# A causal mask moved to another engine, keys and queries stored by head pairs: a two-layer attention trunk on one core

## The chip, the cores and the metric

The kernel runs on one core of a Trainium2 chip. The metric is the device time of one execution in microseconds (us), and the time of a kernel is the median over its runs. Where the text speaks of the span, that is the time from the first to the last instruction in the profile of one execution.

The engines are called as the profile calls them: PE (matrix products and transposes), PEld (PE's loading of weights), DVE (vector operations), ACT (activations and copies), POOL (a second vector engine), SP (which here only issues transfers). A small q behind a name (SPq) is the engine's sequencer, and an instruction there keeps no datapath busy.

## The reference, cut to what matters

Each of two layers is a pair of token mixers followed by a gated feed-forward part with a short convolution. The change lies in the mixers. Mixer B is stick-breaking attention over four heads of 64 channels and 1024 tokens:

```
z = (q @ k.T) * scale
causal = key_pos < query_pos                    # strictly
log_stay = where(causal, log_sigmoid(-z), 0)
later = reverse_cumsum(log_stay) - log_stay
attn  = where(causal, exp(log_sigmoid(z) + later), 0)
o     = attn @ v
```

So the weight of a key is beta = sigmoid(z) times the product of stay = sigmoid(-z) over all later keys. A masked key has beta 0 and stay 1. Mixer A is softmax attention with a bias that falls with distance: four "near" heads over a window of 128 tokens, and eight "far" heads with strides of 4 and 16. All products are in float32, made from high and low parts (hi, lo), three matmuls for a product of two full numbers.

## The kernel before, in words

**Two streams on PE.** In the mixer a class `Dense` holds the input projections (gates, keys, queries, values) as generators. One *dense step* is six matmuls of 512 columns. A function `attend` runs the attention items in order: sixteen *stick* items (four heads, and for each four blocks of 256 queries, longest first: block 3 down to 0), four *near* items, sixteen *far* items. After each micro-step of an item, `dense.advance(rate)` adds the rate to an account and runs a dense step for each whole one in it. The rates are RATE (by block of the stick item), RATE_N (near) and RATE_T (far). PE's order is the order in which the program writes it. The order on the other engines and on SP's queue is set by the framework's planner, from the times that it expects and from priorities (`high_priority(offset=AHEAD)` goes first); on the chip each engine and each queue then works strictly in that order.

**A stick item.** `score(a)` (L682) makes the scores of 128 queries against all keys up to theirs, in pieces of up to 512 columns, last keys first: two matmuls (L631, L632) into a bank `z` of tag "s", the mask added to the last 128 columns by DVE (L695), sigmoid into `beta` (L696) and sigmoid of the negative into `stay` (L697) on ACT. `scans` (L704) then runs DVE's product scan over `stay` (L710) and multiplies `beta` by it (L714). `turn` (L716) transposes `beta` on PE (L722, `sb_t`, tag "t") and splits the result into hi (`sbh`, ACT, L143) and lo (`sbl`, DVE, L150); `apply` (L726) multiplies with the values into `sb_o` (L735, tag "o"), and at the end of an item `fold` (L646, L647) reads it out. Each tag of banks ("ps", "s", "t", "o") has two buffers. The scores of the next item are made between the micro-steps of the current one. While the first stick items run, block sums for the projections (L1013 to L1022 and their splits) are made on the side.

**Keys and queries.** `pair_near` (L1160) projects the keys (c = 0) and queries (c = 1) of two heads at a time, in two token halves n. Each result is 128 rows (two heads of 64) by 512 tokens, hi and lo, and `keep_kq` (L574) writes it to DRAM: for a key four transfers, for a query six, since the hi part of a query is stored twice (on rows 0 to 63 and 64 to 127). `fetch_row` (L652) brings a block of 256 tokens of one head back with three transfers: keys (hi over lo, 128 rows), query hi (twice, 128 rows), query lo (64 rows); `fetch_whole` (L669) does the same for a near head. Values follow on their own (`fetch_values`). A stick item may start six dense steps (LEAD) after its head's last fetch was written down. For the far heads, `fetch_kq` (L841) brings keys and queries from `tk`; the first item may start LEAD = 6 steps after its fetch, the others LEAD_T = 3.

**Values.** `pair_v` (L1175) projects values channel-first and turns them on PE (L1181, `v_t`, tag "t"); ACT and DVE read the bank out (L1185, L1186).

**Pool.** In the mixer, Pool makes two sums of weight blocks for each pair of projections (L1083, L1084), as soon as the weights `in_a` have landed.

Of the kernel before, what the change touches and what calls it, by code (L numbers as in the profile page):

```python
# [7 lines left out]
F32 = mybir.dt.float32  # L8
F32R = mybir.dt.float32r
I32 = mybir.dt.int32  # L10
BF16 = mybir.dt.bfloat16
AF = mybir.ActivationFunctionType
ALU = mybir.AluOpType
# [3 lines left out]
P = 128  # L17
T = 1024
D = 1024
KD = D // P  # L20
HF = 512
# [19 lines left out]
IN_ORDER = {ET.PE, ET.Activation, ET.DVE, ET.Pool}  # L41
HEAD = 4
SECOND = 0.35
RATE = (1.15, 1.3, 1.4, 1.45)
RATE_N = 0.75
RATE_T = 0.5
PLAIN = 4
EARLY = 3
LEAD = 6
# [8 lines left out]
def f32(ap):  # L58
    return ap.bitcast(F32)
# [3 lines left out]
def trunk_kernel(ctx, tc, x, norm1, w_in, b_gate, w_br, w_o, norm2, w_up, conv_w, conv_b, w_down, norm_f, out, depth=None, probe=None):  # L63
# [16 lines left out]
    pool.memset(eps, EPS)  # L80
    zero = cp.tile([P, 1], F32, name="zero")
    pool.memset(zero, 0.0)
    mask_b = cp.tile([P, P], BF16, name="mask_b")
    base0 = cp.tile([P, 256], BF16, name="base0")
    base2 = cp.tile([P, 256], BF16, name="base2")

# [2 lines left out]
    def masks():  # L89

        t = [sb.tile([P, 256], F32, tag="pt", bufs=PT, name=f"msk{i}") for i in range(3)]
        pool.memset(t[0][:, 0:P], 0.0)
        pool.affine_select(t[0][:, 0:P], t[0][:, 0:P], [[-1, P]], ALU.is_gt, -FAR, base=0, channel_multiplier=1)
        dve.tensor_copy(mask_b, t[0][:, 0:P])
        pool.iota(t[1], [[-1, 256]], base=P, channel_multiplier=1, allow_small_or_imprecise_dtypes=True)
        pool.affine_select(t[1], t[1], [[-1, 256]], ALU.is_ge, FAR, base=P, channel_multiplier=1)
        pool.affine_select(t[2], t[1], [[1, 256]], ALU.is_ge, FAR, base=0, channel_multiplier=-1)
        dve.tensor_copy(base0, t[2])
        rem = sb.tile([P, 256], I32, tag="pt", bufs=PT, name="rem")
        pool.iota(rem, [[-1, 256]], base=256, channel_multiplier=1)  # L100
        one = dve.tensor_scalar(rem, rem, 3, None, ALU.bitwise_and)
        tc.add_manual_dep(one.ins, LAST["g0"], NO_SYNC, reason="in turn")
        dve.tensor_copy(t[0], rem)
        dve.tensor_scalar(t[0], t[0], FAR, None, ALU.mult)
        LAST["base"] = dve.tensor_tensor(base2, t[1], t[0], ALU.add).ins.name
# [13 lines left out]
    obd = dr.tile([P, 2, T], F32, name="obd")  # L119
    tk = [dr.tile([2, 4, P, 6, 256], F32, name=f"tk{i}") for i in range(2)]  # L120
    tv = [dr.tile([2, 4, P, 2, 256], F32, name=f"tv{i}") for i in range(2)]
    sk = [dr.tile([P, T], F32, name=f"sk{i}") for i in range(8)]
    sq = [dr.tile([P, 2, T], F32, name=f"sq{i}") for i in range(8)]
    sv = [dr.tile([P, KD, P], F32, name=f"sv{i}") for i in range(8)]
    dn = [dr.tile([4, T], F32, name=f"dn{i}") for i in range(2)]

    def bank(tag, name):
        return ps.tile([P, 512], F32, tag=tag, name=name)
# [95 lines left out]
    class Dense:  # L224
# [38 lines left out]
        def fetch(self):  # L263


            def there(i):
                return i < 16 and {"N11" if i else "N10", f"1{i // 8}", f"2{i // 8}"} <= self.done

            def there_v(i):
                return i < 16 and self.near == 4 and {"v1", "v2"} <= self.done  # L270

            def row(j):
                return j < 16 and f"K{j // 4}" in self.done and self.rows >= j - 3

            def row_v(j):
                return j < self.b and self.free[3 - j % 4] >= j // 4

            def whole(v):
                return v < 4 and self.b == 16 and self.rows == 16 and {f"K{4 + v}", f"V{4 + v}"} <= self.done and self.near >= v

            while row(self.b):
                fetch_row(self.b)
                self.at(LEAD, lambda j=self.b: self.done.add(f"FB{j}"))
                self.b += 1
            while row_v(self.bv):
                fetch_values(self.bv)
                self.bv += 1
            while whole(self.n):
                fetch_whole(self.n)
                self.at(LEAD_N, lambda v=self.n: self.done.add(f"FN{v}"))  # L290
                self.n += 1
            while self.kq < self.scored + 2 and there(self.kq):
                fetch_kq(self.kq)
                self.at(LEAD_T if self.kq else LEAD, lambda i=self.kq: self.done.add(f"F{i}"))
                self.kq += 1
            while self.v < self.applied + 4 and there_v(self.v):
                fetch_v(self.v)
                self.v += 1
# [274 lines left out]

    def keep_kq(c, n, u, hi, lo):  # L574

        t = slice(n * HF, (n + 1) * HF)
        for s in range(2):
            rows = slice(64 * s, 64 * s + 64)
            if c:
                for src, kind, up in ((hi, 0, 0), (hi, 0, 64), (lo, 1, 0)):  # L580
                    nc.sync.dma_start(sq[u + s][up : up + 64, kind, t], f32(src[rows]))
            else:
                for src, up in ((hi, 0), (lo, 64)):
                    nc.sync.dma_start(sk[u + s][up : up + 64, t], f32(src[rows]))

    def in_parts(c, scale, hi, lo, x):
        if c:
# [64 lines left out]
    def fetch_row(j):  # L652

        u, qp = j // 4, 3 - j % 4
        if j == 0:
            R["kv"] = sb.tile([P, 2, T], F32R, tag="xa", bufs=4, name="kv")
            R["slots"] = sb.tile([P, 4, 2, 256], F32R, tag="xa", bufs=4, name="slots")
            pool.memset(f32(R["slots"][64:128, :, 1, :]), 0.0)
        t = slice(256 * qp, 256 * qp + 256)
        nc.sync.dma_start(f32(R["kv"][:, 0, t]), sk[u][:, t])  # L660
        nc.sync.dma_start(f32(R["slots"][:, qp, 0, :]), sq[u][:, 0, t])
        nc.sync.dma_start(f32(R["slots"][0:64, qp, 1, :]), sq[u][0:64, 1, t])

    def fetch_values(j):
        u, qp = j // 4, 3 - j % 4
# [2 lines left out]

    def fetch_whole(v):  # L669
        kv = R["kvn", v] = sb.tile([P, 2, T], F32R, tag="xa", bufs=4, name="kv")  # L670
        nc.sync.dma_start(f32(kv[:, 0, :]), sk[4 + v])
        for k in range(2):
            up = (P, 64)[k]
            nc.sync.dma_start(f32(R["slots"][0:up, :, k, :]), sq[4 + v][0:up, k, :].rearrange("p (m c) -> p m c", c=256))
        nc.sync.dma_start(f32(kv[:, 1, :]).rearrange("p (b c) -> p b c", c=P), sv[4 + v])

    def stick_item(dense, u, qp):
# [4 lines left out]
        def score(a):  # L682
            L = P * (2 * qp + a + 1)
            bt = rows[a] = sb.tile([P, T], F32, tag="p4", bufs=4, name="beta")
            if a == 0:
                st[0] = sb.tile([P, 2, T], F32, tag="xa", bufs=4, name="stay")
            sv = st[0][:, a, :]
            for c1 in range(L, 0, -512):
                c0 = max(0, c1 - 512)
                w = c1 - c0  # L690
                z = bank("s", "z")
                scores(z[:, :w], *(q[:, x, a * P : a * P + P] for x in range(2)), k[:, c0:c1])
                with tc.high_priority(offset=AHEAD):
                    if c1 == L:
                        dve.tensor_tensor(z[:, w - P : w], z[:, w - P : w], mask_b, ALU.add)  # L695
                    act.activation(bt[:, c0:c1], z[:, :w], AF.Sigmoid)  # L696
                    act.activation(sv[:, c0:c1], z[:, :w], AF.Sigmoid, scale=-1.0)  # L697
                (SCANS if c1 == L else left).append((shared, bt, sv, c0, c1, L))
            if a:
                SCANS.extend(left)  # L700
                dense.rows += 1
                scans(2)
# [472 lines left out]
    def pair_v(dense, l, g):  # L1175


        def turn(c, n, f):
            tp = bank("t", "v_t")
            for r in range(4):  # L1180
                pe.transpose(tp[:, r * P : (r + 1) * P], f[:, r * P : (r + 1) * P], ident)  # L1181
            tw = tp.rearrange("p (r h c) -> p r h c", r=4, h=2)
            vv = sb.tile([P, 4, 2, P], F32R, tag="ot", name="vv")
            with tc.high_priority(offset=AHEAD):
                act.copy(vv[:, :, :, 0:64], tw)  # L1185
                dve.tensor_tensor(vv[:, :, :, 64:128], tw, f32(vv[:, :, :, 0:64]), ALU.subtract)  # L1186
            for h in range(2):
                if g:
                    there = tv[c][h, :, :, g - 1, n * P : (n + 1) * P].rearrange("r p c -> p r c")
                else:  # L1190
                    there = sv[4 + 2 * c + h][:, 4 * n : 4 * n + 4, :]
                nc.sync.dma_start(there, f32(vv[:, :, h, :]))
            if (c, n) == (1, 1):
                dense.done |= {f"v{g}"} if g else {f"V{u}" for u in range(4, 8)}

        def put(c, n, x, psum, room=None):
            f = x
            if psum:
                f = small("vf")
                act.copy(f.rearrange("p (r j) -> p r j", r=4) if g else f, x)  # L1200
            dense.at(5, lambda: turn(c, n, f))

        off = OFF_VA + 256 * g
        return pair(dense, l, (off, off + P), g > 0, put)
# [892 lines left out]
```

## Time and profile before

| | |
|---|---|
| median of three runs | 2689.2 us (2685.47, 2689.20, 2691.84) |
| profiled execution | 2686.16 us |
| its span | 2684.4 us |
| mean granted clock of PE | 0.996 |
| mixer of layer 1, stick, near, far items | from about 76, 361 and 445 us |
| mixer of layer 2, stick, near, far items | from about 1404, 1685 and 1768 us |

A row of the waits names an engine and what it waited for, with the total, the number of times and the longest in us. A row of a timeline gives start and duration in us, engine, line, operation, what is written and what is read, and in brackets the idle time before it and what ended that. A row of windows gives a stretch in us, the busy time of PE, PEld, DVE, ACT and POOL in it with the number of instructions, the granted share of PE's clock, the busy share of the transfer engines and GB/s. A row of transfers gives tensors, issuing queue, count, size and the median time from issue to landing in us.

### The profile page before, as it was taken

The numbers are of one execution on the slowest core, as the hardware profiler recorded it, in microseconds if no ns is written. First come the engines' busy times: TensorE is split into PE (matmuls) and PEld (weight loads), VectorE is DVE, ScalarE is ACT, GpSimd is POOL, SyncE is SP. The second block draws the span as 40 slices with busy tenths as digits, with TensorE's granted clock in tenths as the row PEclk, the third lists the DMA queues.
The fourth block names the chain that finished last, engine by engine and source line by source line (L and its number), as shares of the span: only waits on it lengthen the run. The fifth ranks groups of instructions, "written<-read, shape, count | busy, mean of one in ns | idle before, by whom it ended". The sixth has DMA issues, their size and how long they took to land.

```text
span 2684.4 us, 36762 instructions
## 1 busy us (share of the span) xinstructions
PE 2633.4 (98%) x12780; PEld 2198.9 (82%) x12780; DVE 2074.2 (77%) x3159; ACT 1340.2 (50%) x2488; POOL 677.0 (25%) x483
## 2 busy tenths in 40 slices
PE   9999999999999999999999999999999999999999
PEld 8787788888888888888888877878888888888888
DVE  6887766685888988897659777667958888898865
ACT  5455566574555554532435455655745555554225
POOL 5311011122233443321161101100321434344210
PEclk9999999999999999999999999999999999999999
DMA  8553587783244444688453546876732444446863
GB/s 259 147 143 112 146 217 211 236 274 111 78 134 157 160 146 149 223 316 321 160 163 91 150 117 164 224 221 223 251 94 72 161 153 146 160 157 250 333 246 121
DMA packets 418917, 482.94 MB, mean 180 GB/s; under 512 B 26420, under 2 KB 336044, under 8 KB 416940
## 3 DMA queue, kind: packets, MB, share of 16 engines
q1 hardware_dynamic: 418716, 480.59, 55.9%
q8 instruction: 101, 1.65, 0.3%
q14 instruction: 84, 0.69, 0.1%
q10 hardware_dynamic: 16, 0.00, 0.0%
HBM read 307.43 MB, written 173.08 MB: 179 GB/s over the span
## 4 chain that ended last, share of the span: by engine, by line
PE 77%; DVE 10%; ACT 3%; DMA 3%; issue 2%; SPq 1%; POOL 0%; DVEq 0%; ACTq 0%; POOLq 0%
PE u_a L984 5%; PE u_a L985 5%; PE u_a L986 5%; PE d_ps L1725 5%; PE d_ps L1726 4%; PE d_ps L1727 4%; PE i_a L984 3%; PE i_a L985 3%; PE i_a L986 3%; PE u_c L985 3%; PE u_c L984 3%; PE u_c L986 3%; PE o_ps L184 2%; PE o_ps L185 2%; PE o_ps L186 2%
## 5 line engine op out<-in xcount | busy, mean ns | idle before, releaser
L150 DVE TENSOR_TENSOR w_lo<-up_a,w_hi 128x512 fp32r<-128x512 f32 x240 | 236.6, 992 | 20.7 <-ACT w_hi L143 20.7
L143 ACT CAST w_hi<-up_a 128x512 fp32r<-128x512 f32 x240 | 149.4, 623 | 184.3 <-PE u_a L985 45.9
L1083 POOL TENSOR_TENSOR u<-in_a 128x512 f32<-128x512 f32 x32 | 48.7, 1523 | 755.5 <-DMA in_a<-in_w_in_dram 154.7
L1733 DVE TENSOR_TENSOR x<-x,d_ps 128x512 f32<-128x512 f32 (+1 forms) x228 | 151.8, 670 | 77.8 <-PE d_ps L1727 76.5
L1464 POOL TENSOR_TENSOR cv<-cv 128x512 f32<-128x512 f32 x88 | 131.8, 1508 | 249.8 <-DVE cv L1459 140.0
L143 ACT CAST w_hi<-in_a 128x512 fp32r<-128x512 f32 x192 | 119.4, 622 | 130.0 <-DVE in_a L1093 35.7
L150 DVE TENSOR_TENSOR w_lo<-in_a,w_hi 128x512 fp32r<-128x512 f32 x192 | 137.4, 716 | 30.8 <-ACT w_hi L143 27.5
L150 DVE TENSOR_TENSOR g<-cv,g 128x512 fp32r<-128x512 f32 x154 | 151.7, 986 | 5.2 <-ACT g L143 2.8
L1725 PE MATMUL d_ps<-gd_in,w_hi 128*128 128x512 f32 (+1 forms) x340 | 130.5, 384 | 2.2 <-ACT w_hi L143 1.3
L1727 PE MATMUL d_ps<-gd_in,w_lo 128*128 128x512 f32 (+1 forms) x340 | 129.8, 382 | 0.0
L1726 PE MATMUL d_ps<-gd_in,w_hi 128*128 128x512 f32 (+1 forms) x340 | 129.8, 382 | 0.0
L984 PE MATMUL u_a<-hh,w_hi 128*128 128x512 f32 x320 | 124.7, 390 | 0.9 <-DVE u L1615 0.9
L985 PE MATMUL u_a<-t_lo,w_hi 128*128 128x512 f32 x320 | 124.5, 389 | 0.0
L986 PE MATMUL u_a<-t_hi,w_lo 128*128 128x512 f32 x320 | 124.5, 389 | 0.0
L986 PE MATMUL u_a<-hh,w_lo 128*128 128x512 f32 x320 | 124.5, 389 | 0.0
L985 PE MATMUL u_a<-hl,w_hi 128*128 128x512 f32 x320 | 124.5, 389 | 0.0
L984 PE MATMUL u_a<-t_hi,w_hi 128*128 128x512 f32 x320 | 124.5, 389 | 0.0
L143 ACT CAST g<-cv 128x512 fp32r<-128x512 f32 x154 | 94.9, 616 | 39.5 <-POOL cv L1464 28.9
L1725 PE MATMUL d_ps<-gd_in,wd 128*128 128x512 f32 (+1 forms) x292 | 113.9, 390 | 0.0
L150 DVE TENSOR_TENSOR w_lo<-w_raw,w_hi 128x512 fp32r<-128x512 f32 x96 | 73.4, 767 | 52.4 <-ACT w_hi L143 45.5
L710 DVE TENSOR_TENSOR_SCAN stay<-stay,zero 128x512 f32<-128x512 f32 (+2 forms) x96 | 101.1, 1063 | 16.6 <-ACT stay L697 16.4
L1727 PE MATMUL d_ps<-gd_in,wd 128*128 128x512 f32 (+1 forms) x292 | 112.8, 386 | 0.0
(397 smaller groups left out, 8545.1 us busy)
## 6 DMA issues: line engine op xcount, KB each, us to landing
gd<-g SPq DMA_DIRECT2D x154, 512.0 KB, 3.5
gd_in<-gd SPq DMA_DIRECT2D x154, 512.0 KB, 6.0
up_a<-in_w_up_dram SPq DMA_DIRECT2D x80, 512.0 KB, 5.5
in_a<-in_w_in_dram SPq DMA_DIRECT2D x64, 512.0 KB, 5.4
t_kq<-tk SPq DMA_DIRECT2D x32, 768.0 KB, 5.5
wd_raw<-in_w_down_dram SPq DMA_DIRECT2D x22, 1024.0 KB, 11.9
gin<-gs SPq DMA_DIRECT2D x32, 512.0 KB, 4.3
w_raw<-in_w_o_dram SPq DMA_DIRECT2D x64, 256.0 KB, 2.9
```

The source lines that it names most:

```text
L143: one = act.copy(hi, src)
L150: two = dve.tensor_tensor(lo, src, f32(hi), ALU.subtract)
L184: pe.matmul(o, lh, rh, start=(first and i == 0), stop=False, skip_group_check=share)
L710: one = dve.tensor_tensor_scan(rev, rev, zero[:, 0:1].to_broadcast([P, c1 - c0]), 1.0 if c1 == L else sv[:, c1 : c1 + 1], ALU.mult, ALU.add)
L984: pe.matmul(o, w[0][:, c], rh, start=(first and i == 0), stop=False, skip_group_check=True)
L985: pe.matmul(o, w[0][:, c], rl, start=False, stop=False, skip_group_check=True)
L986: pe.matmul(o, w[1][:, c], rh, start=False, stop=(last and i == 3), skip_group_check=True)
L1464: return lambda: pool.tensor_tensor(dst, a, b, ALU.subtract)
L1725: pe.matmul(o[:, sub], wh[:, c], gh[:, sub], start=(i == 0 and k in (0, 4, 5)), stop=False, skip_group_check=True)
L1726: pe.matmul(o[:, sub], wh[:, c], gl[:, sub], start=False, stop=False, skip_group_check=True)
L1727: pe.matmul(o[:, sub], wl[:, c], gh[:, sub], start=False, stop=(i == m - 1), skip_group_check=True)
L1733: dve.tensor_tensor(x, x, o[:, sub], ALU.add)
```

## The change

Four things are changed together. The mask is no longer added to z; two selects on Pool set `beta` to 0 and `stay` to 1 above the diagonal, after ACT. Keys and queries are stored in DRAM with two heads in one tensor, [hi or lo, head, channel, token], so that a key or a query is written with two transfers of 128 rows; the fetches read 64-row pieces and put the hi part of a query on both halves themselves. The transposed values go to a bank of tag "o". The rates of dense steps and the lead of the second far fetch are set anew.

```diff
-RATE = (1.15, 1.3, 1.4, 1.45)
+RATE = (1.1, 1.25, 1.35, 1.4)
-RATE_T = 0.5
+RATE_T = 0.6
...
-    mask_b = cp.tile([P, P], BF16, name="mask_b")
...
-        pool.memset(t[0][:, 0:P], 0.0)
-        pool.affine_select(t[0][:, 0:P], t[0][:, 0:P], [[-1, P]], ALU.is_gt, -FAR, base=0, channel_multiplier=1)
-        dve.tensor_copy(mask_b, t[0][:, 0:P])
...
-    sk = [dr.tile([P, T], F32, name=f"sk{i}") for i in range(8)]
-    sq = [dr.tile([P, 2, T], F32, name=f"sq{i}") for i in range(8)]
+    sk = [dr.tile([2, 2, 64, T], F32, name=f"sk{i}") for i in range(4)]
+    sq = [dr.tile([2, 2, 64, T], F32, name=f"sq{i}") for i in range(4)]
...
-                self.at(LEAD_T if self.kq else LEAD, lambda i=self.kq: self.done.add(f"F{i}"))
+                self.at(LEAD_T if self.kq > 1 else LEAD - 2 * self.kq, lambda i=self.kq: self.done.add(f"F{i}"))
...
     def keep_kq(c, n, u, hi, lo):
-        t = slice(n * HF, (n + 1) * HF)
-        for s in range(2):
-            rows = slice(64 * s, 64 * s + 64)
-            if c:
-                for src, kind, up in ((hi, 0, 0), (hi, 0, 64), (lo, 1, 0)):
-                    nc.sync.dma_start(sq[u + s][up : up + 64, kind, t], f32(src[rows]))
-            else:
-                for src, up in ((hi, 0), (lo, 64)):
-                    nc.sync.dma_start(sk[u + s][up : up + 64, t], f32(src[rows]))
+        there = (sq if c else sk)[u // 2][:, :, :, n * HF : (n + 1) * HF]
+        for x, src in enumerate((hi, lo)):
+            nc.sync.dma_start(there[x].rearrange("s r t -> (s r) t"), f32(src))
...
-        nc.sync.dma_start(f32(R["kv"][:, 0, t]), sk[u][:, t])
-        nc.sync.dma_start(f32(R["slots"][:, qp, 0, :]), sq[u][:, 0, t])
-        nc.sync.dma_start(f32(R["slots"][0:64, qp, 1, :]), sq[u][0:64, 1, t])
+        k, q = (y[u // 2][:, u % 2, :, t] for y in (sk, sq))
+        for x in range(2):
+            nc.sync.dma_start(f32(R["kv"][64 * x : 64 * x + 64, 0, t]), k[x])
+        nc.sync.dma_start(f32(R["slots"][0:64, qp]), q.rearrange("x r t -> r x t"))
+        nc.sync.dma_start(f32(R["slots"][64:128, qp, 0, :]), q[0])
...
-        nc.sync.dma_start(f32(kv[:, 0, :]), sk[4 + v])
-        for k in range(2):
-            up = (P, 64)[k]
-            nc.sync.dma_start(f32(R["slots"][0:up, :, k, :]), sq[4 + v][0:up, k, :].rearrange("p (m c) -> p m c", c=256))
+        k, q = (y[2 + v // 2][:, v % 2] for y in (sk, sq))
+        for x in range(2):
+            nc.sync.dma_start(f32(kv[64 * x : 64 * x + 64, 0, :]), k[x])
+        for up, x in ((0, 0), (64, 0), (0, 1)):
+            nc.sync.dma_start(f32(R["slots"][up : up + 64, :, x, :]), q[x].rearrange("r (m c) -> r m c", c=256))
...
                 with tc.high_priority(offset=AHEAD):
-                    if c1 == L:
-                        dve.tensor_tensor(z[:, w - P : w], z[:, w - P : w], mask_b, ALU.add)
                     act.activation(bt[:, c0:c1], z[:, :w], AF.Sigmoid)
                     act.activation(sv[:, c0:c1], z[:, :w], AF.Sigmoid, scale=-1.0)
+                    if c1 == L:
+                        for x, fill in ((bt, 0.0), (sv, 1.0)):
+                            pool.affine_select(x[:, L - P : L], x[:, L - P : L], [[-1, P]], ALU.is_gt, fill, base=0, channel_multiplier=1)
...
-            tp = bank("t", "v_t")
+            tp = bank("o", "v_t")
```

## The prediction

> **What bounds the kernel now.** I read the first part of the page, then busy time by stage, then what TensorE (PE) waited for, then the clock in the windows behind its longest waits. Each matters because only a wait of PE can be won.
>
> ```profile
> span 2684.4 us, 36762 instructions
> PE 2633.4 (98%) x12780; PEld 2198.9 (82%) x12780; DVE 2074.2 (77%) x3159; ACT 1340.2 (50%) x2488; POOL 677.0 (25%) x483
> ...
> 76.00:360.00 284.00, 272.11 (x1349) 224.55 (x1348) 220.38 (x357) 148.38 (x299) 34.77 (x24) 0.99 0.51 141
> 445.00:573.00 128.00, 121.99 (x720) 105.72 (x719) 91.30 (x199) 73.42 (x167) 14.90 (x14) 0.99 0.78 248
> 1404.00:1686.00 282.00, 272.81 (x1359) 225.32 (x1359) 220.85 (x359) 149.03 (x300) 33.62 (x20) 0.99 0.49 135
> 1768.00:1898.00 130.00, 122.59 (x722) 106.23 (x721) 91.83 (x200) 73.85 (x168) 14.87 (x14) 0.97 0.77 244
> ```
>
> PE is busy for 98% of the span: the program is a stream of matmuls, and the change removes none of them. Of the 51 us in which PE is idle, the two stick stages (rows 76 and 1404) hold 11.9 and 9.2, the two far stages (445 and 1768) 6.0 and 7.4. That is all this change can reach: some 34 us, 1.3%. DVE, at 220 of 284 us, is the next engine in the stick stage; Pool, at 35 of 284, has room.
>
> ```profile
> PE z L631 <- DMA t_kq<-tk: 10.5, 2, 5.8
> PE i_c L984 <- ACT u L1106: 5.1, 3, 3.0
> PE z L631 <- DMA kv<-sk: 5.0, 2, 2.5
> PE v_t L1181 <- DVE sbl L150: 4.2, 2, 2.1
> PE z L631 <- ACT stay L697: 3.9, 7, 1.6
> ```
>
> The columns are total us, times, longest. Each of these five rows touches lines that the diff changes or feeds. A wait also costs clock afterwards:
>
> ```profile
> 256.61:260.02 3.41, 1.30 (x9) 0.82 (x9) 3.41 (x5) 1.59 (x3) 0.98 (x1) 1.00 0.11 28
> 260.02:263.43 3.41, 3.41 (x13) 2.73 (x12) 0.52 (x1) 0.00 (x0) 0.00 (x0) 0.50 0.66 180
> 283.91:287.33 3.42, 1.82 (x8) 1.15 (x7) 2.35 (x5) 1.64 (x4) 0.00 (x0) 1.00 0.78 182
> ...
> sum 20.48, PE 16.52 PEld 14.05 DVE 8.07 ACT 5.50 POOL 0.24; mean PE 3.30 PEld 2.81 DVE 1.61 ACT 1.10 POOL 0.05
> ```
>
> The number after the five engines is the granted clock. A window of 3.41 us with 2.11 idle (256.61) is followed by one at half clock; one with 1.60 idle (283.91) is not. The last row sums the five half-clock stretches of the two mixers (from 133.73, 260.02, 478.48, 1584.39 and 1799.43): they hold 16.5 us of PE work, so they lose 8.3 us, 1.5 behind the first `i_c` wait, 3.4 behind the two of `v_t` and 3.4 behind the two of `t_kq`. The page "TensorE: Matmul & The Clock Gate" of the Trainium skill ("Why this matters for your kernels") warns only of gaps above about 3 us; here 2.11 sufficed, so the measurement decides. By the page the two v_t waits below would return no clock, and my sum would be 3.4 us smaller.
>
> **The change part by part, both layers together.**
>
> *Mask.* DVE loses 64 adds, Pool gains 128 selects.
>
> ```profile
> L695 DVE TENSOR_TENSOR z<-z,mask_b x64: 263/289/300, 78.6 to 1669.4; 128x128 f32<-128x128 f32 x64
>   DVE z L695: 58.5, 48
> L93 POOL TENSOR_SCALAR_AFFINE_SELECT msk<-msk x1: 292/292/292, 1.5 to 1.5; 128x128 f32<-128x128 f32 x1
> ```
>
> 64 x 0.289 = 18.5 us leave DVE; 128 x 0.292 = 37.4 us go to Pool, which has about 500 idle in these two stages. The gain is not DVE's time but the order: ACT works in order, and it sat idle 58.5 us until DVE had added the mask. Now ACT reads z as soon as PE has written it, and the z bank (two of them) is free about 0.3 us plus DVE's backlog sooner. Of the 3.9 us in which PE waited for `stay` I take 2.5, since ACT's own two passes over z stay in front of the bank; bounds 0 and 3.9. The `i_c` wait (5.1, and 1.5 of clock) is ACT's copy of `u5` standing behind a cast that waits for DVE's block sums; the mask is only a small part of that backlog. I take 1, nearest to a DVE that is 0.29 us quicker at each of three places; bounds a loss of 2 (the same backlog, with Pool in its way) and a gain of 6.6.
>
> The selects come back behind ACT, in front of the scan. A scan now waits for Pool in addition, and behind it in DVE's queue stand `w_lo` pieces that PE needs. For most items a row is scored far ahead, so this is covered. It isn't for the first rows of a four-block item: the last row is scored only one or two dense steps before the transposes. There are eight such starts.
>
> ```profile
> 293.41 1.29 POOL L1083 TENSOR_TENSOR u<-in_a 128x512 f32<-128x512 f32 x1 [35.82 <-DMA kv<-sv]
> 294.78 1.29 POOL L1084 TENSOR_TENSOR in_a<-in_a 128x512 f32<-128x512 f32 x1
> ...
> 294.74 0.60 ACT L697 ACTIVATE stay<-z 128x512 f32<-128x512 f32 x1
> ...
> 295.37 1.77 DVE L710 TENSOR_TENSOR_SCAN stay<-stay,zero 128x512 f32<-128x512 f32 x1 [1.16 <-ACT stay L697]
> ```
>
> Here `stay` is done at 295.34 and Pool at 296.07: the select would go 0.7 us late, and two of them cost 0.6, so the scan starts 1.3 us later. I charge 3 us in all: this at two of eight starts. Bounds 0 and the rival below.
>
> ```profile
> 254.14 1.29 POOL L1083 TENSOR_TENSOR u<-in_a 128x512 f32<-128x512 f32 x1 [26.70 <-PE v_t L1181]
> 255.51 2.08 POOL L1084 TENSOR_TENSOR in_a<-in_a 128x512 f32<-128x512 f32 x1
> ...
> 254.56 1.95 DVE L710 TENSOR_TENSOR_SCAN stay<-stay,zero 128x512 f32<-128x512 f32 x1 [1.15 <-ACT stay L697]
> ...
> 258.66 0.68 DVE L150 TENSOR_TENSOR sbl<-sb_t,sbh 128x512 fp32r<-128x512 f32 x1
> ...
> 259.40 0.66 PE L1181 MATMUL v_t<-ident,vf 128*128 128x128 f32 x4 [2.11 <-DVE sbl L150]
> ```
>
> Pool and DVE also hinder each other: beside Pool's 1.29 the scan took 1.95 and Pool's next operation 2.08. The page "SBUF — State Buffer" of the Trainium skill ("Who interferes with whom") speaks against the change: a DVE operation with two inputs in SBUF and a Pool operation that reads SBUF exclude each other for the whole instruction. The rows agree. By that rule each of the eight tight starts could lose one more scan, about 1.2 us, and the sum would be some 10 us worse, at the edge of no change.
>
> *Values turned in bank "o" instead of "t".* The rows above show the wait: `v_t` needed the bank that `sbl` was still reading. In "o", of which the running item holds one buffer, the other is free. But the first product of the item, right behind `v_t`, needs the same `sbl`, which ends at 259.34; PE is free at 257.29 (259.40 less 2.11), `v_t` and the first hi product fill some 0.7, and about 1.3 of the 2.11 us could reappear there. The clock dip should go (1.3 is under 1.6), 3.4 us for two. The mask's DVE slot ahead of that scan goes too. I take 6.5 of 7.6; bounds 1.6 and 7.6.
>
> *Keys and queries by pairs.* By the code, 32 calls that keep keys or queries made 4 or 6 issues of 128 KB each, 160 in all, and now make 2 of 256 KB, 64 in all; 32 row fetches gain one issue and 8 whole ones two: 48 fewer in all.
>
> ```profile
> 273.76 1.08 SPq L581 DMA_DIRECT2D sq<-in_a  x2
> ...
> 284.61 0.60 SPq L584 DMA_DIRECT2D sk<-u  x1
> 285.31 0.54 SPq L660 DMA_DIRECT2D kv<-sk  x1
> ...
> 288.23 0.44 PE L631 MATMUL z<-kv,slots 128*128 128x384 f32 x1 [2.49 <-DMA kv<-sk]
> ...
> sq<-kq_h SPq DMA_DIRECT2D x40, 128.0 KB, 2.4
> tv<-vv SPq DMA_DIRECT2D x32, 256.0 KB, 2.6
> ```
>
> SP is in order and issues one in about 0.6 us. From 273.76 to 284.61 (first and last shown) it issues 16 writes ahead of the key fetch that PE then waits for; with pairs there are at most 8 (4.8 us instead of 9.6), and a write of twice the size lands 0.2 us later. The fetch needs to come 2.5 us sooner. I take 4.5 of 5.0; bounds 0 (SP's order is written ahead by the planner, which may leave the fetch last, behind the data of the last write) and 5.0. Elsewhere SP's time costs PE nothing.
>
> *Rates.* Dense steps in the stick stage fall by 0.05 per micro-step, 28 per head, 5.6 per layer; in the far stage they rise by 0.1, 5 per item, 8 per layer; the second far fetch is held one step longer. No work goes, it moves to where the largest wait is:
>
> ```profile
> 284.67 0.39 PE L985 MATMUL i_c<-t_lo,w_hi 128*128 128x512 f32 x1
> 284.89 0.39 PE L986 MATMUL i_c<-t_hi,w_lo 128*128 128x512 f32 x1
> ...
> 473.36 0.55 SPq L844 DMA_DIRECT2D t_kq<-tk  x1
> ...
> 477.95 0.33 PE L631 MATMUL z<-t_kq 128*128 128x128 f32 x1 [4.75 <-DMA t_kq<-tk]
> ...
> 561.20:573.20 12.00, 4.94 (x12) 2.26 (x12) 1.00 0.80 285
> ```
>
> The load, issued late behind a run of `tk` writes that the change leaves alone, takes 4.6 us to land. Two more dense steps ahead of this item (six matmuls each, 0.22 apart by the first two rows: 1.3 us) would cover 2.6 of 4.75, but the stick stage also hands over its units 5.6 steps later, so the writes may meet another item. Of 10.5 + 3.4 of clock I take 5; bounds a gain of 13.9 and a loss of 4. At the end 12 first-of-three matmuls, six dense steps, cover the join (last row); about 2.6 are left, which is in that loss.
>
> *At the start* the mask's build goes, two Pool operations and a DVE cast. DVE's next step in the chain waited for ACT, not for them, so 0:
>
> ```profile
> 5.99 0.16 DVE L1946 RECIPROCAL ss<-ss 128x1 f32<-128x1 f32 x1 [0.64 <-ACT ss L1945]
> ```
>
> **Sum:** -2.5 - 1 + 3 - 6.5 - 4.5 - 5 = -16.5. The profiled execution took 2686.2 (span and 1.8 around it), so 2669.7. The median of the three runs is 3.0 above the profiled one; I add that: **2673**.
>
> **The rivals.**
> 1. *The waits change places* (0.20). `sb_o` waits for the same `sbl`, the fetch stays last in SP's queue, the far load meets the writes one item later. What is left is 2.5 + 1.6 less some 1: 2686, within 0.2%. For it: the waits recur in both layers at the same step, so they come from an order, and orders are redone here.
> 2. *The far wait goes whole* (0.20): 9 more, and the `i_c` wait halves: 3 more. 2661.
> 3. *Pool becomes the gate* (0.14), slower. Pool is in order, and L1083 waits at its head up to 35.8 us for its data. If the planner puts selects behind it at a tight start, the scan waits 2.6 + 0.6 us and PE with it, and 1.7 of clock follows: 4.9 each. It decides from 16.5 / 4.9 = four of eight starts; at five, with a Pool operation held by DVE at each (0.8, from 2.08 against 1.29), 5 x 5.7 - 16.5 = +12, so 2701. Against it: Pool is busy 35 of 284 us in the stick stage (first fence), so a pair of its operations rarely meets a start.
> 4. *The writes and waits stay as they were for PE*, since every cover above is one that the planner may undo: that is rival 1 at its end, 2689, and has no chance of its own.
>
> The forecast has 0.46, alone 2664 to 2682. The range takes in rival 2 and most of rival 1: **2655 to 2694**. 0.2% is 5.4 us, about what a measurement of this kernel can tell from no change: faster 0.66, same 0.20, slower 0.14.
>
> **What would show it.** Right: no ACT wait for a mask, 128 selects of about 0.3 us; the rows `v_t <- DVE sbl` and `z <- DMA kv<-sk` gone, with no half clock at their places; the `t_kq` row about half. Wrong: new rows `sb_t <- DVE beta` of over 1 us, DVE's scan waiting for Pool, or a `sb_o` wait of over 2 us. A planner that reorders DVE around the scans would upset all of it.

## The result, and the profile after

The changed kernel takes 2664.1 us (median of four runs, 2658.9 to 2665.8) against 2687.3 of the kernel before (four runs, 2684.2 to 2691.8). The ratio is 0.9909, with a 95% interval of 0.9888 to 0.9930: 23 us faster, where 16 were forecast (2673, range 2655 to 2694). The profiled spans differ by 22.0 us.

The first lines of the page after; the line numbers below L570 are smaller by about 4 than before, those further down by 6 to 10 (`z` is L621, `beta` L687, `stay` L688, the selects L691):

```profile
span 2662.4 us, 36856 instructions
PE 2628.7 (99%) x12780; PEld 2195.4 (82%) x12780; DVE 2070.3 (78%) x3094; ACT 1338.6 (50%) x2488; POOL 733.9 (28%) x609
```

PE makes the same 12780 instructions. It is busy 4.7 us less and idle 17.3 us less (2684.4 - 2633.4 = 51.0 before, 2662.4 - 2628.7 = 33.7 after). Where, the windows by stage tell. The bounds are the first transpose of a stick item and the first product with values of a near or far item; idle is the length less the first number after it. Before:

```profile
87.20:372.16 284.96, 274.91 (x1375) 228.01 (x1373) 221.23 (x372) 150.79 (x309) 30.21 (x20) 0.99 0.51 140
372.16:456.80 84.64, 82.34 (x461) 69.81 (x459) 57.78 (x134) 51.59 (x126) 8.65 (x7) 1.00 0.79 214
456.80:1413.56 956.76, 947.30 (x4451) 790.14 (x4450) 749.61 (x1044) 450.35 (x774) 295.24 (x207) 1.00 0.56 187
1413.56:1696.04 282.48, 273.85 (x1374) 227.11 (x1373) 221.31 (x371) 150.54 (x309) 33.62 (x20) 0.99 0.49 137
1696.04:1780.30 84.26, 82.58 (x460) 69.88 (x459) 57.63 (x133) 51.60 (x127) 8.65 (x6) 1.00 0.78 213
1780.30:2684.40 904.10, 889.54 (x4177) 741.64 (x4175) 713.92 (x1000) 436.35 (x751) 251.24 (x173) 1.00 0.54 185
```

And after:

```profile
85.75:352.48 266.73, 263.58 (x1332) 219.37 (x1331) 217.64 (x339) 147.00 (x302) 57.38 (x78) 0.99 0.48 140
352.48:439.48 87.00, 83.01 (x452) 69.70 (x451) 56.29 (x132) 51.57 (x125) 7.76 (x6) 0.98 0.79 206
439.48:1400.51 961.03, 956.16 (x4498) 797.33 (x4497) 753.73 (x1046) 453.70 (x783) 298.84 (x213) 1.00 0.55 188
1400.51:1665.34 264.83, 262.16 (x1332) 218.34 (x1331) 217.39 (x338) 147.04 (x302) 60.42 (x78) 1.00 0.44 133
1665.34:1753.33 87.99, 83.18 (x453) 69.79 (x451) 55.85 (x132) 50.51 (x124) 8.08 (x6) 0.98 0.79 204
1753.33:2662.40 909.07, 898.44 (x4225) 748.71 (x4223) 717.93 (x1004) 440.13 (x759) 250.06 (x173) 1.00 0.54 186
```

The two stick stages are 18 us shorter each, but most of that is work moved: PE is busy 11 to 12 us less in each, and 9 more in each of the far stretches. What is gained is idle time: 18.7 became 5.8 in the stick stages, 24.0 became 15.5 in the two stretches that begin with the far items, and the near items lost 4.8 (4.0 became 8.8). With 0.7 at the start that makes the 17.3. Most of the 4.7 us of busy time is clock:

```profile
133.42:136.84 3.42, 3.42 (x12) 2.73 (x11) 2.93 (x7) 0.92 (x2) 0.00 (x0) 0.50 0.08 21
375.77:379.18 3.41, 3.09 (x9) 2.46 (x9) 2.91 (x6) 1.24 (x3) 0.00 (x0) 0.50 0.81 193
1689.90:1693.31 3.41, 3.41 (x12) 2.75 (x12) 2.01 (x5) 0.62 (x1) 0.00 (x0) 0.50 0.77 175
```

Three half-clock stretches instead of the five (six windows) of before hold 9.9 us of PE work (3.42, 3.09 and 3.41) instead of 16.5, and lose 5.0 instead of 8.3. Idle time and clock make 20.6 of the 22.0 us; the other 1.4 are not accounted for. What PE waits for now (total us, times, longest):

```profile
PE o L796 <- ACT p0h L139: 5.3, 3, 3.0
PE z L621 <- DMA t_kq<-tk: 5.1, 5, 1.5
PE i_c L978 <- ACT u L1100: 3.2, 2, 1.9
PE z L622 <- DMA slots<-sq: 1.9, 3, 0.9
PE z L621 <- ACT stay L688: 1.2, 1, 1.2
```

Of the five rows of the prediction, `kv<-sk` and `v_t <- sbl` are gone, `t_kq` is half, `stay` a third, `i_c` two thirds. Two rows are new: `p0h` at the first near item, in both layers with a half clock behind it (375.77 and 1689.90), and `slots<-sq` for the whole fetches. At the first near item, ACT does this:

```profile
371.76 0.62 ACT L139 CAST w_hi<-in_a 128x512 fp32r<-128x512 f32 x1 [2.87 <-POOL in_a L1078]
...
374.90 0.97 ACT L139 CAST p0h<-t 128x512 fp32r<-128x512 f32 x2
```

The start of a pair of projections falls into the start of the near items. ACT stands 2.87 us until Pool's sum of weight blocks is there, and the cast of that sum stands ahead of the exponentials and `p0h`, which PE waits 2.03 us for. Which of the four edits brings this is told by the experiments, not by this view.

### The profile page after: what moved, and what is told of

Its sections match the earlier page's. It is cut to its first block, busy times and chain, and to the rows that moved or that the text cites. A ratio compares the mean times of both kernels' runs of the same rounds, so it can differ in the third digit from the quotient of the medians.

```text
span 2662.4 us, 36856 instructions
## 1 busy us (share of the span) xinstructions
PE 2628.7 (99%) x12780; PEld 2195.4 (82%) x12780; DVE 2070.3 (78%) x3094; ACT 1338.6 (50%) x2488; POOL 733.9 (28%) x609
## 4 chain that ended last, share of the span: by engine, by line
PE 80%; DVE 10%; DMA 4%; ACT 2%; issue 2%; SPq 1%; POOL 1%; DVEq 0%; ACTq 0%; POOLq 0%
PE u_a L978 5%; PE u_a L980 5%; PE u_a L979 5%; PE d_ps L1719 5%; PE d_ps L1721 4%; PE d_ps L1720 4%; PE i_a L978 4%; PE i_a L980 3%; PE i_a L979 3%; PE u_c L979 3%; PE u_c L980 3%; PE u_c L978 3%; PE o_ps L181 2%; PE o_ps L180 2%; PE o_ps L182 2%
## 5 line engine op out<-in xcount | busy, mean ns | idle before, releaser
L146 DVE TENSOR_TENSOR w_lo<-up_a,w_hi 128x512 fp32r<-128x512 f32 x240 | 237.4, 996 | 20.5 <-ACT w_hi L139 20.5
L691 POOL TENSOR_SCALAR_AFFINE_SELECT beta<-beta 128x128 f32<-128x128 f32 x64 | 31.8, 497 | 306.3 <-ACT beta L687 306.3
```

The source lines that it names most:

```text
L146: two = dve.tensor_tensor(lo, src, f32(hi), ALU.subtract)
```

## The experiments

Four edits are told apart: *mask* (Pool's selects), *DRAM* (keys and queries by pairs), *bank* (`v_t` in "o") and *rates* (RATE, RATE_T and the lead). Eight kernels have one of them alone, or all but one. A ratio is always to the kernel before, with its 95% interval, from five rounds. The theory drawn from the two profiles: the mask and the rates carry the gain, and the rows that the prediction gave to the bank and the layout went because the rates move the projections. The rivals: each part gains what its step said, and the sum is right for its reasons; or no part gains alone, and only the new order as a whole does.

### One edit alone

The edits are the parts of the diff shown above; nothing else differs.

> The kernel before with the mask alone moved to Pool's selects. Theory (each part takes away its own waits, and they add up): the rows z <- ACT stay (3.9 us) fall to about 1.2 and i_c <- ACT u from 5.1 to about 3.2, all others stay; 4 to 5 us less, ratio 0.998. Rival (the parts only work through a new order of everything): other rows move by several us and the time lands anywhere within 0.5%. Rival (Pool becomes the gate): waits of sb_t on DVE's beta of over 1 us, and slower.

> The kernel before with only the layout of keys and queries in DRAM and its transfers changed. Theory of parts: z <- DMA kv<-sk (5.0 us) gone, at most 2 us of a new wait for slots<-sq in the near items, whose whole fetches come in five pieces instead of three; 3 to 5 us less, ratio 0.9985. Rival of the order: the near and far waits move as well.

> The kernel before with only the turned values in bank o. Theory of parts: v_t <- DVE sbl (4.2 us) gone and with it two half-clock windows (3.4 us), but sb_o waits up to 1.3 us each for the same sbl, since the mask on DVE is still there; 4 to 7 us less, ratio 0.998. Rival (the wait only changes its name): sb_o <- DVE sbl of about 2 us at the same two places, half clock behind them, no change of time.

> The kernel before with only the rates and the lead of the second far fetch changed. Theory of parts: t_kq (10.5 us) about halved, the two half-clock stretches behind it gone (3.4), the far items' waits for p1h and p1l (2.9) nearly gone, and a new wait of the near items for p0h of about 6 us with half clock behind it; 4 to 6 us less, ratio 0.998. Rival (the rates bring most of the gain): 12 us or more less, ratio 0.995 or lower.

| alone | median us | ratio | 95% |
|---|---|---|---|
| mask | 2677.95 | 0.9966 | 0.9955 to 0.9978 |
| DRAM | 2690.18 | 1.0015 | 1.0007 to 1.0024 |
| bank | 2688.96 | 1.0010 | 1.0001 to 1.0019 |
| rates | 2675.82 | 0.9960 | 0.9946 to 0.9974 |

Two expectations missed here: DRAM alone, put at 3 to 5 us less, takes 4 more, and the mask, put at 4 to 5, gains 9 (6 to 12 by the interval). For the bank, the rival came. The rates land between theory and rival, nearer the rival, and without the expected wait of about 6 us for `p0h` (it is 0.4).

The bank alone gains nothing: the row of `v_t` is gone, and this one stands in its place (PE's waits, then DVE's and PE's timeline around the first of the two, bank alone):

```profile
PE sb_o L735 <- DVE vv L1186: 4.8, 2, 2.4
```
```profile
259.63 0.68 DVE L1186 TENSOR_TENSOR vv<-v_t,vv 128x512 fp32r<-128x512 f32 x1
...
257.48 0.60 PE L1181 MATMUL v_t<-ident,vf 128*128 128x128 f32 x4
260.45 0.38 PE L735 MATMUL sb_o<-sbh,kv 128*128 128x256 f32 x1 [2.37 <-DVE vv L1186]
```

`v_t` runs at once, but the item's next product needs a bank of the same tag, and DVE reads `v_t` out only at 259.63, behind `sbl`. DVE's queue is as late as before, so PE waits 2.37 instead of 2.11, and the half clock behind it stays. That is rival 1 of the prediction, with a neighbouring operation of the same queue. DRAM alone does remove `kv<-sk`, and pays with a new wait of the same size in the near items, with a half-clock window behind each of the two (from 419.85 and 1744.22; PE's waits, DRAM alone):

```profile
PE t L787 <- DVE vv L1183: 5.2, 2, 2.6
```

The rates alone remove `v_t <- sbl` and `kv<-sk` without touching banks or layout. In PE's waits of that kernel the far wait has halved. `stay` is there as before, and two rows are new: `gt`, and `sb_t <- vv`, as large as the `v_t` row that is gone and again a wait for DVE's late reading of turned values:

```profile
PE z L631 <- DMA t_kq<-tk: 4.6, 3, 2.1
PE i_c L984 <- ACT gt L1226: 4.6, 2, 3.5
PE z L631 <- ACT stay L697: 4.4, 9, 1.6
PE sb_t L722 <- DVE vv L1186: 4.0, 2, 2.2
```

The mask alone removes most of the `stay` row (3.9 to 1.2) and of the `i_c <- u` row (5.1 to 1.3), and two others grow: `i_b <- u` from 1.3 and `sb_t <- beta` from 0.2 (PE's waits, then one row of DVE's timeline, mask alone):

```profile
PE i_b L981 <- DVE u L1114: 4.2, 2, 2.3
PE sb_t L719 <- DVE beta L711: 3.0, 2, 1.8
```
```profile
292.99 1.23 DVE L707 TENSOR_TENSOR_SCAN stay<-stay,zero 128x512 f32<-128x512 f32 x1 [3.49 <-POOL stay L694]
```

`sb_t <- beta` is the row that the prediction named as the sign of Pool being late, and here Pool is late: both selects go behind a pair of weight sums that ends at about 292.4, DVE stands idle 3.49 us, and PE waits 1.14 us at 295.45. The same happens in layer 2 (1.85 us at 1618.05). The edit gains 9 us all the same, by its ratio. Its profiled execution is the slowest of its six (2681.1) and shows only 5 of them.

### All but one

> The changed kernel with the mask back on DVE. Theory (mask and rates carry the gain, about 9 and 11 us alone): z <- ACT stay back at about 4 us, i_c <- ACT u back; 8 to 10 us more than the changed kernel, 2673, ratio to before 0.995. Rival (only the whole set works): 15 us or more are lost, 2680 or above.

> The changed kernel with keys and queries stored by single heads as before. Theory (the fetch wait is removed by the rates already): within 3 us of the changed kernel, 2661 to 2667, without slots<-sq waits of 1.9 us. Rival (the transfers gain only beside the other parts): kv<-sk comes back with about 5 us, 2669 or above.

> The changed kernel with the turned values in bank t as before. Theory (the v_t wait is gone through the rates, the bank is worth nothing by itself): within 3 us of the changed kernel, but a wait like sb_t <- DVE vv of about 2 us each, seen with the rates alone, may come back: up to 2671. Rival (the bank is worth what I forecast, 6.5 us): 2670 or above by v_t <- DVE sbl.

> The changed kernel with the rates and the lead of before. Theory: t_kq back at about 10 us with half clock, v_t or sb_o waits back at about 4, no p0h wait in the near items; 10 us more than the changed kernel, 2674. Rival (the other three parts alone give the forecast for them, 2.5 + 1 + 6.5 + 4.5): 2671 to 2673 with v_t and kv<-sk waits gone. Rival (the parts hinder each other): 2680 or above.

| left out | median us | ratio | 95% | worth in the set |
|---|---|---|---|---|
| mask | 2674.72 | 0.9962 | 0.9949 to 0.9976 | 0.0053, 14 us |
| DRAM | 2664.55 | 0.9920 | 0.9904 to 0.9936 | 0.0011, 3 us |
| bank | 2660.55 | 0.9903 | 0.9889 to 0.9918 | -0.0006, -2 us |
| rates | 2679.53 | 0.9974 | 0.9966 to 0.9983 | 0.0065, 17 us |

The last column is the ratio less 0.9909; each carries about 0.0025 (7 us), both intervals added in squares. So mask and rates are worth something in the set, and of bank and DRAM nothing can be told from zero in this way. The expectations held to within 2 us for mask, DRAM and bank, but for one row: without the mask edit `i_c <- u` was to come back, and it is 0.5. Without the rates 2674 was expected and 2679.5 came. Without the rates the bank's price shows again (PE's waits, all but the rates): `v_t` is read out late, and now a near item pays too.

```profile
PE o L796 <- DVE vv L1180: 4.8, 2, 2.6
PE sb_o L729 <- DVE vv L1180: 4.1, 2, 2.0
```

Without the mask edit, copies of the gates come late. One row of PE's waits, then rows of ACT's and PE's timelines, all but the mask:

```profile
PE i_c L981 <- ACT gt L1223: 5.0, 2, 3.9
```
```profile
1438.00 0.60 ACT L693 ACTIVATE beta<-z 128x512 f32<-128x512 f32 x1 [3.54 <-DVE z L692]
...
1448.03 0.62 ACT L143 CAST hh<-h_sum 128x512 fp32r<-128x512 f32 x1 [2.58 <-DVE h_sum L1019]
1448.56 0.58 ACT L1223 COPY gt<-g_ps 128x512 f32<-128x512 f32 x1
...
1449.19 0.79 PE L981 MATMUL i_c<-t_hi,w_hi 128*128 128x512 f32 x1 [3.88 <-ACT gt L1223]
```

At 1438.00 ACT has stood 3.54 us until DVE reached the mask. Ten us later PE waits 3.88 for a copy of the gates, and that copy stands on ACT behind a cast that waited for a block sum of DVE, not for the mask. With the mask on Pool this row is 0.3; that the earlier wait for the mask makes the later block sums late is not shown.

### Mask and rates together

The kernel before with these two edits, old bank and old layout.

> The kernel before with the mask on Pool and the new rates, but with the old bank and the old DRAM layout. Theory (mask and rates carry the whole gain, bank and layout add nothing in the set): as fast as the changed kernel or a little faster, 2658 to 2666, ratio 0.989 to 0.992; the waits of v_t for sbl and of z for kv<-sk stay gone, since the rates alone removed them. Rival A (the parts only add up as they did alone): -8.2 for the mask and -10.6 for the rates give 2668, 0.993. Rival B (bank or layout is needed for the last part of the gain, and each hid the lack of the other in the two kernels that left one out): 2671 or more, 0.994 or more.

Measured: 2667.47, ratio 0.9934 (0.9922 to 0.9947). The theory that the two carry the whole gain missed; the plain sum of the two alone (2668) hit. From here to the kernel with everything but the bank (0.9903) is what the DRAM layout brings: 0.0031 with some 0.0019 of uncertainty, 8 us with 5. The same layout cost 4 us alone.

PE's idle time by stages, from one profiled execution of each kernel and with the bounds of the windows above (both layers together, us), shows what each edit does where:

| kernel | stick | near | from the far items on |
|---|---|---|---|
| before | 18.7 | 4.0 | 24.0 |
| mask | 18.7 | 1.8 | 22.0 |
| DRAM | 13.3 | 9.9 | 22.1 |
| bank | 20.5 | 3.1 | 23.4 |
| rates | 16.7 | 4.6 | 17.2 |
| mask and rates | 12.4 | 4.7 | 16.2 |
| all but the mask | 13.4 | 7.5 | 15.7 |
| all but DRAM | 10.1 | 2.8 | 14.4 |
| all but the bank | 7.4 | 7.0 | 15.3 |
| all but the rates | 10.5 | 10.6 | 21.0 |
| all four | 5.8 | 8.8 | 15.5 |

Three pairs of these kernels differ in the layout alone (before and DRAM, mask and rates and all but the bank, all but DRAM and all four). In each, the layout takes 4.3 to 5.4 us out of the stick stages and puts 2.3 to 6.0 into the near items. Every kernel of this table with the layout has 7.0 us or more there, and every one without it 4.7 or less; half clock in the near items comes only with the layout. So the near wait of the changed kernel belongs to the layout. Its row is called `t <- vv` (5.2 with DRAM alone, 3.5 in all but the bank), `o <- vv` (4.8 in all but the rates) or `p0h`, as bank and rates have it. Whether it comes from the whole fetches in five pieces or from the order on DVE and ACT is open.

One of the waits left in this kernel shows the rival *Pool becomes the gate* at work (timelines of ACT, Pool, DVE and PE, mask and rates):

```profile
286.88 0.59 ACT L691 ACTIVATE stay<-z 128x512 f32<-128x512 f32 x1
...
289.07 1.62 POOL L1081 TENSOR_TENSOR in_a<-in_a 128x512 f32<-128x512 f32 x1
...
290.89 0.29 POOL L694 TENSOR_SCALAR_AFFINE_SELECT stay<-stay 128x128 f32<-128x128 f32 x1
...
291.21 1.60 DVE L707 TENSOR_TENSOR_SCAN stay<-stay,zero 128x512 f32<-128x512 f32 x2 [1.67 <-POOL stay L694]
...
294.72 0.68 DVE L1120 TENSOR_TENSOR u<-u,i_a 128x512 f32<-128x512 f32 x1
...
295.45 0.50 PE L981 MATMUL i_a<-hh,w_hi 128*128 128x512 f32 x1 [1.96 <-DVE u L1120]
```

`stay` was ready at 287.47. Both selects stood behind a pair of weight sums, the scan came at 291.21 after 1.67 of idle time, and behind the scan stood the addition that frees PE's bank. PE lost 1.96, and half clock followed from 296.26. In the changed kernel PE waits for the same line 0.7 us at most.

### Each select twice

```diff
-                        for x, fill in ((bt, 0.0), (sv, 1.0)):
+                        for x, fill in ((bt, 0.0), (sv, 1.0)) * 2:
```

> The changed kernel with each of Pool's selects done twice (the second changes no value): 128 more, by the row of the changed kernel 0.29 us after beta and 0.52 on average for stay, so 52 us more on Pool. Theory (Pool is not the gate, a row is scored far ahead of its scan): within 0.2% of the changed kernel, 2660 to 2669; DVE waits longer for Pool (22.9 us before this edit, up to some 50), PE's idle time grows by less than 4. Rival (the selects already stand on the path at the tight starts): eight starts of at least 0.8 us more each, and half of them with 1.7 us of clock behind, 6.4 to 13, so 2671 to 2678, with new rows sb_t <- DVE beta on PE.

Measured: 2672.10, ratio 0.9951 (0.9938 to 0.9965), 0.0042 above the changed kernel, 8 us by the spans (2670.8 against 2662.4). The rival's size came, not its rows: there is no `sb_t <- beta`. DVE's wait for Pool grew from 22.9 us (27 times) to this, and PE's idle time in the stick stages from 5.8 to 11.4 (DVE's waits, then the two stages by windows, selects twice):

```profile
DVE stay L704 <- POOL stay L691: 37.1, 35, 3.3
```
```profile
86.39:356.90 270.51, 264.84 (x1333) 219.17 (x1332) 219.65 (x339) 147.26 (x302) 81.01 (x137) 0.99 0.47 138
1405.70:1674.40 268.70, 263.02 (x1332) 218.10 (x1331) 219.85 (x338) 146.98 (x302) 83.43 (x137) 1.00 0.44 131
```

It is spread over several rows, most with waits of under 1.5 us each and most for DVE. So Pool has little room left, although in the changed kernel it is busy only 57 of 267 us there.

### Stay ahead of beta on ACT

```diff
-                    act.activation(bt[:, c0:c1], z[:, :w], AF.Sigmoid)
                     act.activation(sv[:, c0:c1], z[:, :w], AF.Sigmoid, scale=-1.0)
+                    act.activation(bt[:, c0:c1], z[:, :w], AF.Sigmoid)
                     if c1 == L:
-                        for x, fill in ((bt, 0.0), (sv, 1.0)):
+                        for x, fill in ((sv, 1.0), (bt, 0.0)):
```

> The changed kernel with ACT's two passes exchanged: stay first and beta second, and the selects in the same order, so that Pool sets stay's mask while ACT makes beta. PE's order is unchanged. Theory (doubling Pool's selects cost 8 us through DVE, which came to wait 14 us longer for Pool; so the 22.9 us that DVE still waits for Pool's stay cost PE something too): that row falls under 10 us, the idle time of PE in the two stick stages (4.1 and 4.7 us in the changed kernel) falls by 1 to 3 in all, and the time is 2656 to 2662. Rival (one pass of selects is covered, only the second was not): the row of DVE falls as well, but the time stays at 2662 to 2668. The 5.3 us for p0h in the near items (and the two half clocks behind it) have another cause and stay.

Measured: 2661.53, ratio 0.9911 (0.9897 to 0.9924), against 0.9909 of the changed kernel. DVE's wait fell, to 13.4 and not below 10 (DVE's waits, stay first):

```profile
DVE stay L704 <- POOL stay L691: 13.4, 22, 2.3
```

PE's idle time in the stick stages did not fall (7.1 against 5.8). The time itself lies in the range of the theory (2656 to 2662), but the ratio is that of the changed kernel, and 1 to 3 us are less than these ratios can tell. By PE's idle time the rival holds: in the changed kernel one pass of selects is covered. The second pass is not, and the theory drawn from it does not reach back to the first. The `p0h` row stayed, at 3.6 us, with gaps of 1.68; the half clock behind it, which was expected to stay, went.

### The stick rates alone

```diff
-RATE = (1.15, 1.3, 1.4, 1.45)
+RATE = (1.1, 1.25, 1.35, 1.4)
```

> The kernel before with the four stick rates alone lowered by 0.05; far rate and second far lead as before. Theory (the stick rates carry the gain of the rates, by moving the projections against the stick items): rows v_t <- sbl (4.2) and z <- kv<-sk (5.0) gone, with the 3.4 us of clock of the former, so 2674 to 2678, like all rates together (2675.8). Rival (the far rate carries it, by covering the t_kq wait): the stick rows gone but the t_kq wait at 8 us or more, and 2681 or more.

Measured: 2679.25, ratio 0.9977 (0.9968 to 0.9986), between the two expectations. PE's waits, stick rates alone:

```profile
PE z L631 <- DMA t_kq<-tk: 8.1, 4, 3.8
```

`v_t <- sbl` and `kv<-sk` are gone, as with all rates, and 6 us are gained. But `sb_t <- vv` (4.7) and `gt` (4.7) stand in their place, and PE's idle time in the stick stages is 19.1, not less than the 18.7 of before. What fell is the idle time from the far items on (24.0 to 18.1) and the half clock behind the two `v_t` waits (3.4 us). The far wait is 8.1 instead of 4.6 with all rates, so the far rate and the lead together bring 3.5 us more by that row; by the ratios (0.9960 against 0.9977) 5, with as much uncertainty.

## Why the prediction was right in its total, and where its steps failed

**What bounds the kernel** was right: the gain is PE's idle time and clock, 20.6 of 22.0 us, nearly all of it in the mixers.

**The mask was mis-sized.** The step for `stay` was right: the row went from 3.9 to 1.2 (2.7; 2.5 forecast), it is 1.2 with the mask alone too, and 4.4 without this edit. The step for `i_c <- u` names a row that does not stay put: 5.1 before, 1.3 with the mask alone, 0.5 in the kernel without the mask edit and 3.2 in the changed one. All waits of PE for `i_c` (`u`, `gt` and `kq_l`) are 6.6 us without this edit and 3.5 with it. The edit was put at a net gain of 0.5, after 3 us for Pool, and is worth 9 us alone and 14 with about 7 of uncertainty in the set. The working priced two rows, and left out that the order on ACT and DVE changes for everything behind the mask. In the set that shows in the copies of gates (`i_c <- ACT gt`, 5.0 us without this edit, 0.3 with it), and in all in 7.6 us of PE's idle time in the stick stages. Alone it is not located: in the profile of that kernel the stick stages are as idle as before (18.7), since `i_b` and `sb_t` took 5.7 of the 6.5 us that `stay` and `i_c` gave. The charge of 3 us for Pool, at two of eight starts, was right for the mask alone, where `sb_t <- beta` takes 3.0 us at two places behind a pair of Pool's sums; in the changed kernel the row is not there. That Pool can be the gate is shown once more with mask and rates (1.96 us and a half clock at one place) and where its selects are doubled (8 us).

**The port rule** (the page "SBUF — State Buffer" of the Trainium skill, "Who interferes with whom") would have added some 10 us. The selects do run slower beside DVE, and a loss of that size did not come. Two groups of Pool's instructions, by form, after (busy us and mean ns behind the bar):

```profile
L691 POOL TENSOR_SCALAR_AFFINE_SELECT stay<-stay 128x128 f32<-128x128 f32 x64 | 33.2, 519 | 3.9 <-ACT stay L688 3.3 <-DMA sq<-kq_h 0.2
L691 POOL TENSOR_SCALAR_AFFINE_SELECT beta<-beta 128x128 f32<-128x128 f32 x64 | 31.8, 497 | 306.3 <-ACT beta L687 306.3
```

They take 65.0 us, not the 37.4 of 128 x 0.292: 0.51 on average, where the prediction's sign was about 0.3. The 51 selects with no DVE instruction beside them take 0.29 each (0.288 to 0.297), the 73 beside a DVE scan or operation on two tensors 0.67 on average and up to 2.45. That agrees with the rule in its direction.

**Values in bank "o": the step failed.** It put 6.5 us on a wait for a bank. The wait was for DVE's queue, and any bank that DVE must read is as late; alone the edit costs 2.7 us, and leaving it out of the set makes 2 us less, with 7 of uncertainty. The text had seen that the product behind `v_t` needs the same `sbl`, and priced only 1.3 us of it, since it left out that DVE's read of `v_t` itself then stands between the item and its bank.

**Keys and queries by pairs: the step was right where it looked, and left out the near items.** The row `kv<-sk` went, by fewer issues as described, and the stick stages lose 4.3 to 5.4 us of idle time in each of the three pairs of kernels (4.5 forecast). What the step put at nothing ("Elsewhere SP's time costs PE nothing") is the near items: 2.3 to 6.0 us more idle time there, and half clock. Alone that leaves a loss of 4 us; on top of mask and rates, where the near items pay least (2.3), a gain of 8 with 5 of uncertainty; in the set with the bank 3 with 7. For the last pair the profiled executions say the opposite of the ratios (2656.9 without the layout, 2662.4 with it), but the kernel without it spreads from 2658.6 to 2671.0 and its fastest execution was the profiled one. So this stays open.

**The rates were mis-sized, 5 for 11 to 17.** In the changed kernel the far wait fell by 5.4 and the far half clocks went (3.4), 8.8 of the 13.9 that could be had there; the rates alone leave one of these half clocks, at 1803.60. PE's idle time from the far items on falls by 5.5 to 6.8 us wherever the rates are added, close to the 5 forecast, and by 5.9 with the stick rates alone. The rest is in the stick stages, 2.0 us alone, 6.3 beside the mask and 4.7 in the set, and in the half clock behind the `v_t` waits. There the step held the stick rates for mere moving of work. They decide which dense unit meets which item: `v_t <- sbl` and `kv<-sk` went, but alone nearly as much came back under other names.

The total was right by luck. The bank's 6.5 us did not come and the near items cost what no step had, while mask and rates together brought 18 instead of the 5.5 of their terms; these errors cancel. Alone the four make -9.1 + 4.0 + 2.7 - 10.8 = -13 us by their ratios, and together -24. Mask and rates nearly add (-20 as a sum, -18 measured); bank and layout cost 7 us as a sum and bring 7 on top of these two. Why they gain there is shown in part only: without the bank, the near items pay less for the layout than when it stands alone (2.3 us against 5.9).

**The rivals.** The waits did change places where bank or layout stood alone. *The far wait goes whole* did not come. *Pool becomes the gate* came at single places only. One sign that the prediction named for being wrong did come, DVE's scan waiting for Pool (22.9 us in 27 waits, the longest 3.9; before, the scans waited 16.4 us for `stay` from ACT), but PE did not pay for it. The prediction also added 3.0 us for the distance of the median from the profiled execution; after the change that distance is 0.0 (2664.07 and 2664.06). And the near wait of 5.3 us, with 3.3 us of half clock, stood in no step: it comes with the layout, whose term should have asked for it.

None of the tried variants beats the changed kernel beyond doubt: the ratios without the bank edit (0.9903) and with stay first (0.9911) lie within its interval.

## What to carry to other kernels

A wait that ends with a late in-order queue is not won by another buffer: ask what the engine has to do next for the same consumer, and price that. A row of waits that is gone is not yet a gain, since its time may stand under another name; compare the idle time of the whole stage. Gains of edits that meet in the same queues need not add, in either direction; run each alone and each left out before one is credited. An engine that is busy a fifth of the time can still stand at the head of the path when its instructions are in order behind a pair of long ones.

## What the runs showed of the hardware

**The half clock depends on the idle sum of a fixed 3.41 us window, not on one gap.** With stay first PE waited 2.25 us at 130.82, but the wait straddles two windows, and no half clock followed (the window that holds most of it and the one behind, stay first):

```profile
131.26:134.67 3.41, 1.60 (x7) 1.29 (x8) 3.41 (x8) 3.24 (x8) 1.22 (x2) 1.00 0.19 54
134.67:138.08 3.41, 3.41 (x21) 2.93 (x20) 3.41 (x7) 1.60 (x3) 0.00 (x0) 1.00 0.09 23
```

1.81 idle in the window is not enough; the 1.96 of mask and rates at 292.85 was. In each of the fourteen profiles of this case the half-clock stretches begin whole multiples of 3.413 us apart, to within 2 ns. Taking windows on that grid, those at full clock with 1.92 us or more idle were all followed by half clock, and between 1.85 and 1.92 both happened. With less than 1.85 none was, but for four at the very end, the last window in which PE works, with 1.58 to 1.84.

**Most of the larger DRAM writes landed sooner, two groups later.** The prediction took 0.2 us more for 256 KB than for 128 KB. Before, each group of writes of keys or queries had a median of 2.4 us from issue to landing. After, with 128 rows instead of 64 in a write, those of `u`, `in_a` and the query's `kq_h` take 2.0 to 2.1 us, but those of `kq_l` 4.7 for queries and 4.9 for keys (rows of transfers, after: size, median us):

```profile
sq<-kq_h SPq DMA_DIRECT2D x10, 256.0 KB, 2.0
sq<-kq_l SPq DMA_DIRECT2D x10, 256.0 KB, 4.7
```

Why `kq_l` is later stays open.
